# Layer 0's last two experts returned by float32 one-hot products, and layer 1's in-chunk S5 matrix loaded behind its norms

## The chip, the core and the metric

One Trainium2 chip, one of its cores. The time is that of one execution on the device in microseconds (us). TensorE is called PE here (its weight loads PEld), VectorE DVE, ScalarE ACT, GpSimd POOL; SyncE (SP) issues most DMAs. Weights lie in device memory (HBM) and are streamed through SBUF; products are summed in PSUM.

## What is computed

The reference is a two-layer backbone over 256 latent tokens and, in layer 0, 256 context tokens (512 in all, four tiles of 128), 1024 wide:

```
for l in range(2):
    h  = rms_norm(x, norm1_g[l]) * (1 + mod[1]) + mod[0]
    o  = token_mixers(h, ...)            # attention, S5, Fourier: w_in, w_out
    x  = x + mod[2] * o
    h2 = rms_norm(x, norm2_g[l]) * (1 + mod[4]) + mod[3]
    x  = x + mod[5] * moe_ffn(h2)        # 16 experts, each token takes 2
def moe_ffn(t):
    for e in range(16):
        he = silu(t @ w_gate[e]) * (t @ w_up[e])
        y  = y + gates[:, e:e+1] * (he @ w_down[e])
```

What matters here is the end of layer 0's experts (layer 0 handles the context rows as well) and the start of layer 1: x must have both experts' rows, times gate and mod[5], before rms_norm of layer 1 can begin. S5 is a state-space mixer; within chunks of eight time steps it is a product with a fixed matrix made from the layer's S5 parameters.

## The kernel before

The program is written as one stream of instructions in Python; a scheduler sets the order on each engine, by program order among what it expects to be ready, and places the semaphores. `issue_after(x)` binds the instructions of a block to stand behind x on x's own engine. A tile of a pool waits until the last user of its slot is done.

Layer 0's experts are `experts0` (L1569 to L1722). Each expert takes up to 96 gathered tokens ("rows"). For expert e the loop does the gate and up products (eight k-steps, `steps`, out tiles g and u, PE in four column groups), SiLU times up (tile s, L1653 to L1660), three transposes of s (T, L181), a copy to H, and the down product (py, tiles y). The k-steps 0 to 2 of e+1 are put around the transposes of e, so PE has work in the gaps. Each expert's weights come as six pieces of 1 MB (four of gate and up, two of down) that SP issues in order (`wseq`, L1460 and L1463) into nine to thirteen slots; at most eight of these DMAs are under way, each on a semaphore of its own.

Rows go back in this way. Experts 0 to 14: py is copied to y and stored by POOL to a DRAM table Y (L1701, L1702). At the start of expert 15 POOL gathers from Y for each token tile T and for each of the token's two experts the row by an indirect DMA (L1649, eight of them, into weight slots, `rg`). `others(T)` (L1610) scales the two rows by the gates, adds them, multiplies by mod[5] (tile B5) and adds to X[T]: one ACT and three DVE operations, for T = 2 the last two on POOL. Expert 15 itself doesn't go through Y: its rows of Y are zeros (L646), y is split in two float32r halves (`split`), and `combine0` (L1724) returns them by one-hot products with OG, for each T, then times gate and B5 on DVE, added to X. OG is made after expert 14 (L1715 on): a comparison on DVE, a transpose and three small products on PE, two copies on DVE, for each T. `others` for all T stands in program order behind expert 15's y.

`normed` (L397) then takes X[T] tile by tile: square on ACT (L389), a line of DVE, a power on POOL (L394, kept as `self.pow`), the scaling on ACT (L404). `combine0` is called through it, and after each T it also takes steps of `fill`, which loads w_ada and multiplies it (tiles E). Then `mixers(1)` loads w_in (L303) and starts its products A.

Spread over experts 7 to 14 of layer 0, `s5_prep(1)` (L923) makes layer 1's S5 matrices; its in-chunk matrix is written to DRAM (KD) and is to be read back to tile MT by eight DMAs of POOL (`inchunk`, L1051 to L1054, 128 KB each). For layer 1, `inchunk` is called in `mixers` (L508), behind the first projection; nothing binds it to stay there. MT is read in `s5_out`.

Of the kernel before, what the change touches and what calls it, by code (L numbers as in the profile page):

```python
# [14 lines left out]
OP = mybir.AluOpType  # L15
# [119 lines left out]
class Net:  # L135
# [66 lines left out]
    def run(self):  # L202
        nc, A, t = self.nc, self.A, self.t
        with ExitStack() as st:
# [60 lines left out]
            with ExitStack() as s2:  # L265
                last = self.experts0(s2)
            lay.close()
            with ExitStack() as s1:
                with ExitStack() as s2:
                    self.open_psum(s1, s2, 1)  # L270
                    self.open_b(1, "left")
                    self.fill = self.fills(1)
                    self.combine0(*last)
# [133 lines left out]
    def mixers(self, l, sa, sb):  # L407
# [99 lines left out]
        if not both:  # L507
            self.inchunk()  # L508
# [122 lines left out]
        for sh, hp in self.attention(QT, KT, V, MX, BM):  # L631
            if both and sh == 0:
                next(fill, None)
                zi = next(zero, None)
                if zi is not None:
                    nc.gpsimd.dma_start(zi, z[:, None, :].to_broadcast([P, 6, 512]))
            elif both:
                next(nada)
            else:
                next(fill, None)  # L640
                if sh:
                    next(first)
                elif hp == 3:
                    self.fetch(1)
            if both and (sh, hp) == (0, 3):
                nc.gpsimd.dma_start(self.Y[NROW - 96:NROW, :].rearrange("p (a h) -> p a h", a=2),  # L646
                                    z[0:96, None, :].to_broadcast([96, 2, 512]))
# [538 lines left out]
    def route_open(self, l):  # L1186
# [25 lines left out]
        if l == 0:  # L1212
            self.gi = t(pm, [P, 2, nt], "gi", U32)
            self.le = t(pm, [P, 2, nt], "le")
# [22 lines left out]
    def route_tile(self, l, T):  # L1237
# [140 lines left out]
        nc.vector.tensor_copy(self.le[:, 0, T:T + 1], pos[:, NE - 1:NE])  # L1378
        nc.gpsimd.tensor_copy(self.le[:, 1, T:T + 1], GT[:, NE - 1:NE])
# [189 lines left out]
    def experts0(self, st):  # L1569
# [40 lines left out]
        def others(T):  # L1610

            w = rg[T]
            nc.scalar.activation(w[:, 0], w[:, 0], AF.Copy, scale=self.ga[:, 0, T:T + 1])
            nc.vector.scalar_tensor_tensor(w[:, 0], w[:, 1], self.ga[:, 1, T:T + 1], w[:, 0], op0=OP.mult, op1=OP.add)
            v = nc.gpsimd if T == 2 else nc.vector
            v.tensor_tensor(w[:, 0], w[:, 0], B5[T // 2], op=OP.mult)
            v.tensor_tensor(self.X[T], self.X[T], w[:, 0], op=OP.add)
# [9 lines left out]

        xg0, xg = gather(1, nc.sync), None
# [3 lines left out]
        for e in range(NE):  # L1632
# [38 lines left out]
            cp = self.cp(H, pt, 0)  # L1671
            if e == 0:
# [14 lines left out]
            yr = [(slice(0, cap), n, slice(0, YM), slice(512 * n, 512 * n + YM)) for n in range(2)]  # L1687
            yr += [(slice(96, P), n, slice(0, 2 * mt - mt * n), slice(2 * mt * n, 2 * mt + mt * n)) for n in range(2)]
            if e == NE - 1:
# [8 lines left out]
            for i, (r, n, c, d) in enumerate(yr):  # L1698
                self.cp(y[r, d], py[n][r, c], (0, 1, 1, 0)[i])
            Y = self.Y[e * cap:e * cap + cap, :]  # L1700
            nc.gpsimd.dma_start(Y[:, 0:2 * YM].rearrange("r (h c) -> r h c", h=2), y[:cap, :].rearrange("p (h c) -> p h c", h=2)[:, :, 0:YM])  # L1701
            nc.gpsimd.dma_start(Y.rearrange("(b i) c -> i b c", i=32)[:, :, 2 * YM:D],  # L1702
                                y[96:128, 0:3 * mt].rearrange("p (b c) -> p b c", b=3))
            for _ in range(2 if prep else 0):
                with self.tc.issue_after(act.ins), self.tc.issue_after(mul.ins):
                    done = next(prep, prep) is prep
                if done and fin is None:


                    fin = self.fin = self.open(self.finx, "fin", side="right")  # L1710
                    OG = t(fin, [P, 3, 4, P], "OG", F32R)
                    B5 = [self.bcast(fin, "B5", 5, s, 2) for s in range(2)]
                    for T in range(4):
                        og = t(fin, [P, 96], "og")
                        nc.vector.tensor_scalar(og, self.iota, self.le[:, 0, T:T + 1], None, op0=OP.is_equal)  # L1715
                        pt = t(psT, [P, 3, P], "T")
                        self.tr(pt[0:96, 0, :], og)
                        for b in range(3):
                            self.mm(pt[96:128, b, :], og[:, blk(b)], self.ident, True, True)
                        self.cp(OG[0:96, 0, T, :], pt[0:96, 0, :], 0)  # L1720
                        self.cp(OG[96:128, :, T, :], pt[96:128], 0)
        return y, OG, B5  # L1722

    def combine0(self, y, OG, B5):  # L1724

        nc, t = self.nc, self.t

        def add(T):
            mt = D - 2 * YM
            ps = [t(self.psA, [P, YM], "A"), t(self.psA, [P, YM], "A"), t(self.psT, [P, mt], "T")]  # L1730
            for n in range(2):
                for i in range(2):
                    self.mm(ps[n], OG[0:96, 0, T, :], y[i][0:96, 512 * n:512 * n + YM], i == 0, i == 1)
            for b in range(3):
                for i in range(2):
                    self.mm(ps[2], OG[96:128, b, T, :], y[i][96:128, mt * b:mt * b + mt], b + i == 0, b + i == 3)
            for n in range(3):
                c = slice(n * YM, min(n * YM + YM, D))
                w = t(self.tmp, [P, 512], "w2")[:, 0:c.stop - c.start]
                nc.vector.scalar_tensor_tensor(w, ps[n], self.le[:, 1, T:T + 1], B5[T // 2][:, c], op0=OP.mult, op1=OP.mult)  # L1740
                nc.vector.tensor_add(self.X[T][:, c], self.X[T][:, c], w)
            for _ in range((2, 1, 1, 1)[T]):
                next(self.fill)
        self.normed(add)
# [209 lines left out]
```

## Time and profile before

| | us |
|---|---|
| median of 3 runs | 1128.43 (1128.0 to 1131.83) |
| profiled execution, its own time | 1127.95 |
| its span, first to last instruction | 1126.2 |
| PE busy | 1035.6 (92%) |
| DVE busy | 606.4 (54%) |
| ACT busy | 305.5 (27%) |
| POOL busy | 168.9 (15%) |

The profiled execution's own time lies 1.75 us above its span and 0.48 us below the median. All times in rows are counted from the span's start. "[0.46 <-DMA w]" behind a row says that the engine had been idle for 0.46 us before it, and what ended that. A matmul of float32 operands shows as two records, one of float32r operands as one.

### The profile page before, as it was taken

The page shows a single profiled execution, that of the slowest core. Times are in us where ns is not written, and L with a number is a line of the kernel's source. Part 1 is how long each engine was busy: PE and PEld are TensorE (multiplying, and loading weights), DVE is VectorE, ACT ScalarE, POOL GpSimd, SP SyncE. Part 2 cuts the span into 40 slices and gives each one's busy share as a digit, 9 for nine tenths or more (in the row PEclk, how much of TensorE's full clock was granted, in tenths as well). Part 3 has the DMA queues.
Part 4 walks back from the last instruction along what each step waited for, and adds up shares of the span by engine and source line. Part 5 has one row for each costly group of instructions (what it writes and reads, how often), then busy time and mean ns, then how long its engine had stood idle before and what let it go on. Part 6 is the DMA issues. An engine that isn't in the chain of part 4 may idle for free.

```text
span 1126.2 us, 21063 instructions
## 1 busy us (share of the span) xinstructions
PE 1035.6 (92%) x8496; PEld 651.8 (58%) x8496; DVE 606.4 (54%) x1691; ACT 305.5 (27%) x619; POOL 168.9 (15%) x255
## 2 busy tenths in 40 slices
PE   4999998989989999898987889999999899999987
PEld 2667775548885655455654447767558455444533
DVE  8978937568742222297633396695468423232322
ACT  5323234564101111101111136322473221111211
POOL 3101233001223111111220330104010100000000
PEclk9999999999969999999998968999999999999999
DMA  9868576756479999999999646644868899999981
GB/s 312 297 224 220 174 277 249 237 181 243 149 302 278 372 365 377 380 387 372 381 309 367 237 176 243 226 158 161 282 218 294 337 400 401 387 396 403 401 340 40
DMA packets 109393, 325.25 MB, mean 289 GB/s; under 512 B 10704, under 2 KB 19632, under 8 KB 104672
## 3 DMA queue, kind: packets, MB, share of 16 engines
q1 hardware_dynamic: 94464, 276.01, 67.2%
q0 software_dynamic: 14096, 46.57, 12.7%
q8 instruction: 71, 1.16, 0.4%
q10 hardware_dynamic: 720, 1.17, 0.3%
q14 instruction: 42, 0.34, 0.1%
HBM read 305.32 MB, written 18.38 MB: 287 GB/s over the span
## 4 chain that ended last, share of the span: by engine, by line
PE 56%; DMA 23%; DVE 10%; issue 5%; POOL 3%; ACT 3%; SPq 1%; another core or an unknown queue 0%; POOLq 0%; ACTq 0%; DVEq 0%
PE A L157 22%; DMA w<-in_w_up_dram 14%; PE g L157 12%; PE D L157 8%; PE E L157 5%; DMA w<-in_w_gate_dram 5%; PE T L181 4%; PE T L157 2%; PE y L157 2%; DMA w<-in_w_down_dram 1%; PE u L157 1%; POOL qr L752 1%; DMA X<-in_xt_dram 1%; DVE wsp L199 1%; DMA w<-in_w_ada_dram 1%
## 5 line engine op out<-in xcount | busy, mean ns | idle before, releaser
L157 PE MATMUL g<-w,xt 128*32 128x384 f32 (+1 forms) x1280 | 164.4, 456 | 16.4 <-DMA w<-in_w_gate_dram 12.4
L157 PE MATMUL A<-wsp,big 128*128 128x512 f32 (+1 forms) x720 | 161.8, 371 | 3.1 <-DVE big L190 2.0
L157 PE MATMUL u<-w,xt 128*32 128x384 f32 (+1 forms) x1024 | 138.4, 468 | 8.8 <-DMA w<-in_w_up_dram 8.8
L157 PEld LDWEIGHTS A<-wsp,big 128*128 128x128 f32 x720 | 121.1, 188 | 40.1 <-ACT wsp L189 7.5
L157 PEld LDWEIGHTS g<-w,xt 128*32 128x32 f32 x1280 | 70.1, 111 | 63.2 <-issue 33.5
L157 PE MATMUL y<-w,H 128*32 128x384 f32 (+1 forms) x1152 | 89.6, 459 | 1.3 <-DVE H L190 1.3
L157 PE MATMUL g<-w,x 128*64 128x512 f32 x384 | 90.6, 594 | 0.0
L157 PEld LDWEIGHTS u<-w,xt 128*32 128x32 f32 x1024 | 57.5, 112 | 36.7 <-issue 9.8
L157 PE MATMUL E<-w,CS 128*32 128x512 f32 (+1 forms) x448 | 63.2, 589 | 14.4 <-DMA w<-in_w_ada_dram 14.0
L157 PEld LDWEIGHTS y<-w,H 128*32 128x32 f32 x1152 | 52.9, 111 | 34.4 <-issue 12.2
L1893 DVE TENSOR_TENSOR cst<-cst,g 64x512 f32<-64x512 f32 x16 | 11.1, 692 | 111.7 <-ACT cst L1892 111.7
L199 DVE TENSOR_TENSOR wsp<-w,wsp 128x512 fp32r<-128x512 f32 x64 | 43.9, 687 | 44.8 <-ACT wsp L189 43.7
L189 ACT ACTIVATE wsp<-w 128x512 fp32r<-128x512 f32 x64 | 40.4, 631 | 98.8 <-PE A L157 90.3
L157 PE MATMUL A<-w,big 128*128 128x512 f32 (+1 forms) x224 | 67.0, 391 | 0.0
L189 ACT ACTIVATE y<-y 96x384 f32<-96x384 f32 (+4 forms) x34 | 17.9, 531 | 163.2 <-PE y L157 147.4
L1654 DVE TENSOR_TENSOR s<-s,u 96x384 f32<-96x384 f32 x16 | 8.8, 551 | 95.1 <-ACT s L1653 95.0
L157 PEld LDWEIGHTS g<-w,x 128*64 128x64 f32 x384 | 28.7, 137 | 49.9 <-issue 47.8
L1848 DVE SCALAR_TENSOR_TENSOR y<-D,gs,ba 64x256 f32<-64x256 f32 x62 | 30.0, 483 | 45.5 <-PE D L157 44.7
L1598 POOL DMA_DIRECT2D xg<-G x56 | 30.5, 551 | 136.1 <-DVE xt L1605 106.4
L157 PEld LDWEIGHTS A<-w,big 128*128 128x128 f32 x224 | 41.0, 192 | 7.7 <-issue 0.5
L157 PE MATMUL D<-w,WO 128*64 128x256 f32 x352 | 44.2, 393 | 1.1 <-ACT WO L189 1.1
L1892 ACT ACTIVATE cst<-g 64x512 f32<-64x512 f32 x16 | 9.4, 589 | 101.5 <-PE g L157 101.5
(415 smaller groups left out, 1721.8 us busy)
## 6 DMA issues: line engine op xcount, KB each, us to landing
w<-in_w_gate_dram SPq DMA_DIRECT2D x111, 512.0 KB, 13.0
w<-in_w_up_dram SPq DMA_DIRECT2D x111, 512.0 KB, 12.6
w<-in_w_down_dram SPq DMA_DIRECT2D x53, 1024.0 KB, 12.7
w<-in_w_ada_dram SPq DMA_DIRECT2D x27, 1024.0 KB, 6.9
w<-in_w_in_dram SPq DMA_DIRECT2D x14, 1024.0 KB, 5.2
w<-in_w_ada_dram SPq DMA_DIRECT2D x32, 256.0 KB, 6.6
w<-in_w_ada_dram SPq DMA_DIRECT2D x16, 512.0 KB, 4.8
w<-in_w_out_dram SPq DMA_DIRECT2D x8, 1024.0 KB, 7.4
```

The lines of the kernel that those rows point to most:

```text
L157: self.pe = self.pl = self.nc.tensor.matmul(out, lhsT, rhs, start=start, stop=stop)
L181: self.pl = self.nc.tensor.transpose(out, in_, self.ident[:n, :n])
L189: return self.nc.scalar.activation(out, in_, AF.Copy)
L199: self.lo = self.nc.vector.tensor_tensor(lo, x, hi.bitcast(F32), op=OP.subtract)
L752: nc.gpsimd.tensor_tensor(r, v, self.neghalf[:, 0:8], op=OP.pow)
L1598: q.dma_start(xg[blk(g)], rows[g])
L1654: nc.vector.tensor_mul(s[:cap, :], s[:cap, :], pg[1][:cap, 0:384])
L1848: nc.vector.scalar_tensor_tensor(y[o:o + 64, m, b, :], py[m][q, :], gs[q, e % 2:e % 2 + 1], B5[q, m, :], op0=OP.mult, op1=OP.mult)
L1892: nc.scalar.activation(s[64:P], pg[0:64], AF.Silu)
L1893: nc.vector.tensor_mul(s[64:P], s[64:P], pg[64:P])
```

## The change

- At layer 1's `mixers`, `inchunk()` (the eight loads of MT) is bound to stand behind the last `self.pow` on POOL, the power of layer 1's fourth norm.
- Experts 14 and 15 of layer 0 are both kept out of Y: their y stays in SBUF as float32 (`late`), with the last quarter of the columns moved to the same partitions as the rest. Expert 14's two stores on POOL fall away; rows of both experts in Y are zeros, so there is a second zero store early in layer 0.
- OG is float32, two one-hots for each T (one for each of the two experts), with the gate already multiplied in; a transpose each, one copy on ACT for both. The three small products and the DVE copies fall away.
- The gathers thus need Y only up to expert 13. T = 1 takes the slot that T = 3 had. `others(0)` and `others(1)` stand at the start of expert 15; `others(2)` and `others(3)` stand behind expert 15's H copy (DVE) and SiLU (ACT), all on DVE.
- The return products `back(i, T)` (two float32 products of 96 x 128 by 96 x 512, for late expert i = 0, 1): `back(0, 0)` stands on PE between expert 15's up product and the transposes of s, `back(0, 1)` between these and the down product, `back(0, 2)` behind the down product, then `back(1, T)`, with `back(0, 3)` ahead of `back(1, 3)`. DVE multiplies by B5 and adds to X, in two halves of 512.
- `combine0` only keeps the norm and `fill`.

```diff
         if not both:
-            self.inchunk()
+            with self.tc.issue_after(self.pow.ins):
+                self.inchunk()
...
-            self.le = t(pm, [P, 2, nt], "le")
+            self.le = t(pm, [P, nt, 2, 2], "le")
...
-            v = nc.gpsimd if T == 2 else nc.vector
-            v.tensor_tensor(w[:, 0], w[:, 0], B5[T // 2], op=OP.mult)
-            v.tensor_tensor(self.X[T], self.X[T], w[:, 0], op=OP.add)
+            nc.vector.tensor_tensor(w[:, 0], w[:, 0], B5[T // 2], op=OP.mult)
+            nc.vector.tensor_tensor(self.X[T], self.X[T], w[:, 0], op=OP.add)
+
+        def back(i, T):
+
+            for n in range(2):
+                self.mm(acc[T][n], OG[:, i, T, :], late[i][:cap, n * 512:n * 512 + 512], i == 0, i == 1)
...
                 rg = [t(p, [P, 2048], "w").rearrange("p (k n) -> p k n", k=2) for p in (self.ws, self.ws2, self.ws2, self.ws2)]
+                rg = [rg[i] for i in (0, 3, 1, 2)]
                 for T in range(4):
                     for k in range(2):
                         nc.gpsimd.indirect_dma_start(out=rg[T][:, k], out_offset=None, in_=self.Y,
                                                      in_offset=bass.IndirectOffsetOnAxis(ap=self.gi[:, k, T:T + 1], axis=0))
+                for T in range(2):
+                    others(T)
+                acc = [[t(psG, [P, 512], n) for n in "gu"], None, None, None]
...
+            if e == NE - 1:
+                with self.tc.issue_after(self.pe.ins):
+                    back(0, 0)
...
+            if e == NE - 1:
+                acc[1] = [t(psG, [P, 512], n) for n in "gu"]
+                with self.tc.issue_after(self.pl.ins):
+                    back(0, 1)
+                with self.tc.issue_after(cp.ins), self.tc.issue_after(act.ins):
+                    for T in (2, 3):
+                        others(T)
...
-                y = [t(fin, [P, D], f"y{i}", F32R) for i in range(2)]
-                for r, n, c, d in yr:
-                    self.split(y[0][r, d], y[1][r, d], py[n][r, c])
-                with self.tc.issue_after(act.ins), self.tc.issue_after(mul.ins):
-                    for T in range(4):
-                        others(T)
-                break
...
+                late.append(y)
+                for n in range(2):
+                    self.cp(y[:cap, n * YM:n * YM + YM], py[n][:cap, 0:YM], n)
+                for b in range(3):
+                    self.cp(y[blk(b), 2 * YM:D], py[b // 2][96:128, mt * (b % 2):mt * (b % 2) + mt], (0, 1, 1)[b])
...
+                        for i in range(2):
+                            og = t(fin, [P, 96], "og", bufs=2)
+                            nc.vector.tensor_scalar(og, self.iota, self.le[:, T, 0, i:i + 1], self.le[:, T, 1, i:i + 1], op0=OP.is_equal, op1=OP.mult)
+                            self.tr(pt[:cap, i, :], og)
+                        self.cp(OG[:, :, T, :], pt[:cap, 0:2, :], 1)
+
+        acc[2] = [t(psT, [P, 512], "T") for n in range(2)]
+        acc[3] = [t(psY, [P, 512], f"y{n}") for n in range(2)]
+        back(0, 2)
+        for T in range(4):
+            if T == 3:
+                back(0, 3)
+            back(1, T)
             for n in range(2):
...
+                nc.vector.tensor_mul(w, acc[T][n], B5[T // 2][:, c])
                 nc.vector.tensor_add(self.X[T][:, c], self.X[T][:, c], w)
```

## Rows read from the trace of the kernel before

**Rows 1.** The chain that ended last, 540 to 612 us: start, us, what
```profile
556.16 16.38 DMA w<-in_w_gate_dram
...
572.61 24.67 DMA w<-in_w_gate_dram
```

**Rows 2.** Timeline of PE: start, us, what, count, idle before and its releaser
```profile
571.43 0.52 PE L157 MATMUL u<-w,xt 128*32 128x384 f32 x3 [1.38 <-DMA w<-in_w_up_dram]
...
575.95 5.39 PE L157 MATMUL y<-w,H 128*32 128x384 f32 x72
...
597.42 1.50 PE L157 MATMUL g<-w,xt 128*32 128x384 f32 x6 [8.42 <-DMA w<-in_w_gate_dram]
...
604.11 5.39 PE L157 MATMUL y<-w,H 128*32 128x384 f32 x72
```

**Rows 3.** Timeline of POOL, 560 to 650 us: MT's loads, B5, gathers
```profile
572.85 2.82 POOL L1053 DMA_DIRECT2D MT<-KD  x5 [7.23 <-DMA w<-in_w_gate_dram]
...
584.01 1.68 POOL L1053 DMA_DIRECT2D MT<-KD  x3
...
632.67 0.60 POOL L380 DMA_DIRECT2D B<-MD  x1
...
635.98 1.01 POOL L1649 DMA_INDIRECT w<-Y,gi  x1 [2.01 <-PE T L157]
...
644.78 0.94 POOL L1649 DMA_INDIRECT w<-Y,gi  x1 [0.30 <-issue]
```

**Rows 4.** DMA by queue, 576 to 586 us: packets, MB, share of 16 engines
```profile
q1 hardware_dynamic: 360, 1.36, 66.4%
q0 software_dynamic: 239, 0.66, 37.7%
```

**Rows 5.** DMA by queue, 600 to 610 us
```profile
q1 hardware_dynamic: 1076, 4.03, 101.5%
```

**Rows 6.** Timelines of PE and ACT, 629 to 672 us
```profile
629.93 1.09 PE L181 MATMUL T<-cst,LB 128*128 128x128 f32 x8
...
647.69 0.49 ACT L1653 ACTIVATE s<-g 96x384 f32<-96x384 f32 x1 [15.24 <-remote]
...
649.37 0.87 PE L181 MATMUL T<-cst,s 128*128 128x128 f32 x3 [5.34 <-DVE s L1660]
650.89 7.51 PE L157 MATMUL y<-w,H 128*32 128x384 f32 x72 [0.65 <-DVE H L190]
...
670.31 1.06 ACT L389 ACTIVATE w<-X 128x1024 bf16<-128x1024 f32 x1 [9.02 <-DVE X L1741]
```

**Rows 7.** Timeline of DVE: `others(0)`, three operations
```profile
650.87 1.28 DVE L1614 SCALAR_TENSOR_TENSOR w<-w,ga 128x1024 f32<-128x1024 f32 x1
652.18 1.22 DVE L1616 TENSOR_TENSOR w<-w,B 128x1024 f32<-128x1024 f32 x1
653.44 1.23 DVE L1617 TENSOR_TENSOR X<-X,w 128x1024 f32<-128x1024 f32 x1
```

**Rows 8.** Windows: us, busy (count) of PE, PEld, DVE, ACT, POOL; granted clock, DMA share, GB/s
```profile
648.00:658.00 10.00, 7.98 (x74) 4.51 (x75) 8.78 (x10) 4.05 (x6) 0.56 (x1) 0.66 0.51 207
658.00:671.00 13.00, 10.21 (x43) 5.98 (x35) 12.13 (x17) 3.46 (x6) 6.16 (x4) 0.65 0.47 161
```

**Rows 9.** The chain, 1110 to 1126 us: records of whole-array float32 products, 512 wide
```profile
1114.02 1.13 PE A L157 x2
...
1117.24 2.00 PE A L157 x4
```

**Rows 10.** Groups of DVE and timelines, 628 to 690 us: adding to X; norm's end
```profile
L1741 DVE TENSOR_TENSOR X<-X,w 128x384 f32<-128x384 f32 x8 | 4.4, 551 | 0.2
...
673.00 6.32 SPq L303 DMA_DIRECT2D w<-in_w_in_dram  x2
...
681.76 1.15 ACT L404 ACTIVATE U<-X,rstd 128x1024 f32<-128x1024 f32 x1 [0.26 <-POOL rstd L394]
```

More of the change, by code (lines that the diff above doesn't have):

```diff
@@ L265, in run @@
             with ExitStack() as s2:
-                last = self.experts0(s2)
+                self.experts0(s2)
             lay.close()
@@ L272, in run @@
                     self.fill = self.fills(1)
-                    self.combine0(*last)
+                    self.combine0()
                     lay = self.mixers(1, "right", "left")
@@ L645, in mixers @@
             if both and (sh, hp) == (0, 3):
-                nc.gpsimd.dma_start(self.Y[NROW - 96:NROW, :].rearrange("p (a h) -> p a h", a=2),
-                                    z[0:96, None, :].to_broadcast([96, 2, 512]))
+                for i in (1, 2):
+                    nc.gpsimd.dma_start(self.Y[NROW - 96 * i:NROW - 96 * i + 96, :].rearrange("p (a h) -> p a h", a=2),
+                                        z[0:96, None, :].to_broadcast([96, 2, 512]))
         if both:
@@ L1376, in route_tile @@
             return
-        nc.vector.tensor_copy(self.le[:, 0, T:T + 1], pos[:, NE - 1:NE])
-        nc.gpsimd.tensor_copy(self.le[:, 1, T:T + 1], GT[:, NE - 1:NE])
+        nc.vector.tensor_copy(self.le[:, T, 0, :], pos[:, NE - 2:NE])
+        nc.gpsimd.tensor_copy(self.le[:, T, 1, :], GT[:, NE - 2:NE])
         IN, SL = t(bc, [P, NE], "IN"), t(bc, [P, NE], "SL")
@@ L1626, in start @@
             return steps, pg, lambda k: w[k // 2][:, k % 2, :]
+        late = []
         xg0, xg = gather(1, nc.sync), None
@@ L1686, in experts0 @@
             mt = D - 2 * YM
-            yr = [(slice(0, cap), n, slice(0, YM), slice(512 * n, 512 * n + YM)) for n in range(2)]
-            yr += [(slice(96, P), n, slice(0, 2 * mt - mt * n), slice(2 * mt * n, 2 * mt + mt * n)) for n in range(2)]
-            if e == NE - 1:
-                y = [t(fin, [P, D], f"y{i}", F32R) for i in range(2)]
-                for r, n, c, d in yr:
-                    self.split(y[0][r, d], y[1][r, d], py[n][r, c])
-                with self.tc.issue_after(act.ins), self.tc.issue_after(mul.ins):
-                    for T in range(4):
-                        others(T)
-                break
-            y = t(ex, [P, D], "y")
[L1698 to L1703, printed above, removed]
+            y = t(ex, [P, D], "y")
+            if e < NE - 2:
+                yr = [(slice(0, cap), n, slice(0, YM), slice(512 * n, 512 * n + YM)) for n in range(2)]
+                yr += [(slice(96, P), n, slice(0, 2 * mt - mt * n), slice(2 * mt * n, 2 * mt + mt * n)) for n in range(2)]
+                for i, (r, n, c, d) in enumerate(yr):
+                    self.cp(y[r, d], py[n][r, c], (0, 1, 1, 0)[i])
+                Y = self.Y[e * cap:e * cap + cap, :]
+                nc.gpsimd.dma_start(Y[:, 0:2 * YM].rearrange("r (h c) -> r h c", h=2), y[:cap, :].rearrange("p (h c) -> p h c", h=2)[:, :, 0:YM])
+                nc.gpsimd.dma_start(Y.rearrange("(b i) c -> i b c", i=32)[:, :, 2 * YM:D],
+                                    y[96:128, 0:3 * mt].rearrange("p (b c) -> p b c", b=3))
+            else:
+                late.append(y)
[3 more added lines that the diff above has]
+                    self.cp(y[blk(b), 2 * YM:D], py[b // 2][96:128, mt * (b % 2):mt * (b % 2) + mt], (0, 1, 1)[b])
             for _ in range(2 if prep else 0):
@@ L1710, in experts0 @@
                     fin = self.fin = self.open(self.finx, "fin", side="right")
-                    OG = t(fin, [P, 3, 4, P], "OG", F32R)
+                    OG = t(fin, [cap, 2, 4, P], "OG")
                     B5 = [self.bcast(fin, "B5", 5, s, 2) for s in range(2)]
                     for T in range(4):
-                        og = t(fin, [P, 96], "og")
-                        nc.vector.tensor_scalar(og, self.iota, self.le[:, 0, T:T + 1], None, op0=OP.is_equal)
                         pt = t(psT, [P, 3, P], "T")
[L1717 to L1730, printed above, removed]
-            for n in range(2):
[L1732 to L1740, printed above, removed]
+                        for i in range(2):
+                            og = t(fin, [P, 96], "og", bufs=2)
+                            nc.vector.tensor_scalar(og, self.iota, self.le[:, T, 0, i:i + 1], self.le[:, T, 1, i:i + 1], op0=OP.is_equal, op1=OP.mult)
+                            self.tr(pt[:cap, i, :], og)
@@ new lines, in experts0 @@
+                        self.cp(OG[:, :, T, :], pt[:cap, 0:2, :], 1)
[6 more added lines that the diff above has]
+            back(1, T)
+            for n in range(2):
+                c = slice(n * 512, n * 512 + 512)
+                w = t(self.tmp, [P, 512], "w2")
+                nc.vector.tensor_mul(w, acc[T][n], B5[T // 2][:, c])
@@ L1741, in add, with combine0, ready @@
                 nc.vector.tensor_add(self.X[T][:, c], self.X[T][:, c], w)
+    def combine0(self):
+        def ready(T):
             for _ in range((2, 1, 1, 1)[T]):
                 next(self.fill)
-        self.normed(add)
+        self.normed(ready)
         self.finx.close()
```

## The prediction

> **What bounds the kernel now.** I read the chain of waits first, from 540 to 700 us, since the page's shares are means over stages with different limits. Two places on it concern this change.
>
> From 556 us the chain runs over weight transfers; one takes 24.67 us from its issue, where the one before took 16.38 [rows 1]. PE stands still for 8.42 us until the first piece of expert 14 is there [rows 2]. In that time the POOL queue moves MT, issued at 572.85 and 584.01 [rows 3]. From 576 to 586 us the weight queue moved 1.36 MB and the POOL queue 0.66 [rows 4]; undisturbed, the weight queue moves 4.03 MB in 10 us [rows 5]. So MT is paid for in weights, where weights are what PE waits for.
>
> The second place is the joint between the layers. Expert 14's down product ends at 629.93, the first norm begins at 670.31: 40.4 us [rows 6]. In them expert 15 needs 17.8 us to its SiLU, then its down product runs 7.51 us (5.39 in [rows 2]), at a mean clock of 0.66, between the two granted levels of 1.2 and 2.4 GHz [rows 8]. Gathers start only at 635.98 and go on to 645.7 in their issue alone [rows 3]. From 658 to 671 DVE is busy 12.13 of 13 us [rows 8]: the four `others`, y's halves and the additions all come there. So the joint is bound by what was put off to its end, not by PE.
>
> **The change part by part.** *MT's move.* Lost weights from 576 to 586 are 4.03 - 1.36 = 2.67 MB, 6.6 us at the rate of [rows 5]; the three loads issued from 584.01 act again. PE's own loss is the 8.42 us and the slow restart: from 597.42 to the down product at 604.11 are 6.69 us, where expert 13 took 4.52 plus some 0.25 done before its wait [rows 2]. Together 8.42 + 1.9 = 10.3 us at most. Without MT the first pair of expert 14 comes 6.3 MB of weights and 0.4 MB of stores behind that of expert 13, which ended a wait at 571.43; 6.7 MB at 403 GB/s are 16.6 us, 588.1, and PE is ready at 589.0 (597.42 - 8.42). So nearly all is gained; I take 9.5, bounds 7 and 10.3. Behind it PE is its own bound, and SP's later loads wait for PE's slots and shift with it.
>
> At its new place MT's eight issues (4.5 us) stand behind the last power; behind them on POOL come only loads and powers of the projections, tens of us later. Its transfers fall beside w_in's second half and the next w_ada. These are issued at 679.3 and later, when the norms end at 682.91 [rows 10]; in the new order PE's backlog is shorter and slots come free earlier, so I take 1 us, bounds 0 and 7 (the 6.6 us above and a rest).
>
> The Trainium skill (DMA: Bandwidth & Descriptors, Queues, rings and completion order) says that each DMA engine takes turns among the queues with work, packet by packet. The trace agrees: two queues share the engines 66.4 to 37.7 [rows 4]. By that rule MT costs weights wherever a weight load is under way: it is the first rival below.
>
> *The joint.* Count from expert 14's last down product. PE: LB's transposes 1.1 [rows 6]; 90 records of gate and up left, at 5.39/72 each, 6.7 [rows 2]; eight transposes of one-hots, a third of a T row's 0.87 each at most [rows 6], 1.2 taken; waits between DVE, PE and ACT for the one-hots 2, taken (0 to 6: before, the same stretch took 17.8 us for at most 11 of work, and its last 3.6 us have no row). Expert 15's SiLU thus starts at 11.0 instead of 17.8.
>
> Then s needs 1.7 us (647.69 to 649.37), filled by `back(0, 0)`. A return product is two records: (2.00 - 1.13)/2 = 0.435 us each [rows 9], so 0.87, and 1.74 for a `back`. Transposes 0.87; `back(0, 1)` 1.74 covers the H copy, 0.65 (650.24 to 650.89) [rows 6]; down product 5.39 [rows 2], since PE has no gap in which the clock falls: 11.0 + 1.74 + 0.87 + 1.74 + 5.39 = 20.7. `others(2)` and `others(3)` are 3.73 us each on DVE [rows 7] and start with the H copy's end at 14.3, so DVE comes to y at 21.8; its part, 1 us, is done at 22.8, behind `back(0, 2)` at 22.5. `back(1, 0)` ends at 24.5. DVE then has a multiplication and an addition of 512; 0.551 for 384 [rows 10] gives 0.7 each: first norm at 25.9, against 40.4. Later T come each 1.74 us of PE and 2.8 of DVE, the last behind two `back`; before, the four norms take 12.6 us, 670.31 to 682.91 [rows 6, 10], 3.15 each, so PE and DVE stay ahead. `others(0)` and `others(1)`, 7.5 us on DVE, lie beside the gate and up products; they need B5, which can be issued when LB is done, and T = 0 and 1, gathered before expert 14 has ended because their slots are free and Y is only needed to expert 13. The gain is 14.5, bounds 8 (waits of 6 and DVE late) and 18 (no waits).
>
> The Trainium skill (Perfetto Trace Analysis, Engine Utilization) rates the array at 307.2 G outputs a second, halved for FP32_LOW_HIGH. By it a product of 128 x 512 would take 0.43 us, an estimate; the rows show 0.87 for its two records, so the row decides. By the page's figure the first norm would come some 0.9 us earlier.
>
> *The rest.* Expert 14's two stores fall away, the second zero store is one POOL issue of about 0.6 us early in layer 0, beside attention; the two-column copies for `le` cost the same. I take nothing; if that cover is gone it is under 1 us.
>
> Sum: 1127.95 - 9.5 - 14.5 + 1 = 1104.95, say **1105** (the profiled execution's own time; the median lies 0.48 above it). Everything behind the joint shifts as it is: its loads wait on its own slots.
>
> **The rivals.** *MT holds up layer 1.* At the new place the weight queue gets a third of its rate for some 10 us; if w_in's second half or w_ada is still under way, PE waits up to 7 us. For it: two w_in loads are only just issued at the norms' start [rows 10]. Against: PE needs the second half four k-steps later. 1105 + 6 = 1111.
>
> *The one-hots and DVE stay the bound.* DVE runs in order; if `others(0)` waits for B5 ahead of one-hots or of s, PE waits too, and PE's 3.6 us without a row may return. 1105 + 6 = 1111.
>
> *Only one half works.* The gathers stay behind B5 on POOL, as at 632.67 and 635.98 [rows 3], and the joint gains 5 instead of 14.5, or the weights come late without MT too: 1114.
>
> *Slower.* DVE's order is the mechanism: if all four `others` (15 us) stand ahead of s, PE is idle for 15 us from 11.0 on, the clock goes to its lower level, and products behind it (8 x 1.74 + 5.39 = 19.3 us) take twice that: 15 + 19.3 = 34 over the plan, 10 beyond both gains: 1139. It decides from some 24 us of loss. Against: two of the four are bound behind the H copy.
>
> **How the numbers follow.** Forecast 0.58; MT in layer 1 0.16; one-hots and DVE 0.15; one half 0.07; slower 0.04. The forecast's own range is 1098 (10.3 and 18 gained, 1 given back, 1127.95 - 27.3 = 1100.65, less 2.65 for loads that start sooner) to 1109; rivals reach 1114, and with the bounds 7, 8 and 7 together 1120. I leave the corners out: 1098 to 1116. A measurement of this kernel tells about 0.5% (5.6 us) from no change; faster by more is under 1122.8: 0.93, within it 0.03, slower 0.04.
>
> **What would show it.** Right: no POOL MT row before the norms of layer 1; no PE wait of several us at expert 14; four of the gathers issued before expert 14's down product ends; the down product of expert 15 near 5.4 us at full clock; about 26 us from expert 14's last product to the first norm; A products following U's scaling by the 3 us of before. Wrong: PE waits for w_in or w_ada behind the norms, DVE idle in front of `others(0)` with one-hots behind it, or expert 14 still waiting for weights.

## The result, and the profile after

| | kernel before | kernel after |
|---|---|---|
| median (range), us | 1128.2 (1125.7 to 1131.8, 4 runs) | 1111.6 (1109.2 to 1114.4, 4 runs) |
| ratio, 95% interval | 1 | 0.9844 (0.9808 to 0.988) |
| profiled execution: time, span, us | 1127.95, 1126.2 | 1112.08, 1110.3 |

Faster by 16.6 us, inside the range, 6.6 us above the forecast of 1105. The sum is close for a wrong reason: one of its two large terms was a little too small, the other has no shown gain behind it, and in the profiled pair differences between two executions fill the gap.

The timeline of PE in the kernel after (start, us, what, count, idle before and its releaser), from expert 12's down product to expert 15's, against [rows 2] and [rows 6]:

```profile
573.60 5.41 PE L157 MATMUL y<-w,H 128*32 128x384 f32 x72
...
591.19 5.41 PE L157 MATMUL y<-w,H 128*32 128x384 f32 x72
...
611.71 5.39 PE L157 MATMUL y<-w,H 128*32 128x384 f32 x72
617.03 1.09 PE L181 MATMUL T<-cst,LB 128*128 128x128 f32 x8
618.05 0.83 PE L157 MATMUL g<-w,xt 128*32 128x384 f32 x2
622.91 0.42 PE L181 MATMUL T<-cst,og 128*96 128x128 f32 x1 [4.03 <-DVE og L1738]
...
635.20 1.13 PE L157 MATMUL g<-y,OG 96*128 96x512 f32 x2
...
640.03 5.41 PE L157 MATMUL y<-w,H 128*32 128x384 f32 x72
...
648.43 1.02 PE L157 MATMUL g<-y,OG 96*128 96x512 f32 x2
649.29 1.02 PE L157 MATMUL u<-y,OG 96*128 96x512 f32 x2
```

No wait for weights is left: expert 13's product stands 12.9 us earlier than at 604.11 [rows 2], expert 14's ends at 617.1 instead of 630. But behind it PE waits 4.03 us for a one-hot, and expert 15's product comes 22.9 us behind the end of expert 14's; 20.9 before.

POOL, ACT and DVE in the kernel after say why (same columns; a w read from Y is a gathered row block, og a one-hot):

```profile
610.27 1.43 POOL L1658 DMA_INDIRECT w<-Y,gi  x1 [10.99 <-DMA w<-in_w_down_dram]
...
618.41 0.61 POOL L380 DMA_DIRECT2D B<-MD  x1
...
664.86 4.53 POOL L1055 DMA_DIRECT2D MT<-KD  x8
```

```profile
616.40 1.15 ACT L1615 ACTIVATE w<-w,ga 128x1024 f32<-128x1024 f32 x1 [8.02 <-DMA w<-Y,gi]
617.79 1.15 ACT L1615 ACTIVATE w<-w,ga 128x1024 f32<-128x1024 f32 x1 [0.25 <-issue]
619.67 0.88 ACT L189 ACTIVATE y<-y 96x384 f32<-96x384 f32 x2 [0.73 <-PE g L157]
...
634.88 0.49 ACT L1665 ACTIVATE s<-g 96x384 f32<-96x384 f32 x1 [3.20 <-PE g L157]
...
656.57 1.06 ACT L389 ACTIVATE w<-X 128x1024 bf16<-128x1024 f32 x1 [9.20 <-DVE X L1753]
...
664.94 1.15 ACT L404 ACTIVATE U<-X,rstd 128x1024 f32<-128x1024 f32 x1 [0.26 <-POOL rstd L394]
```

```profile
620.34 1.28 DVE L1616 SCALAR_TENSOR_TENSOR w<-w,ga 128x1024 f32<-128x1024 f32 x1 [7.03 <-DMA w<-Y,gi]
621.54 0.98 DVE L190 COPY y<-y 96x384 f32<-96x384 f32 x2
622.45 0.55 DVE L1738 TENSOR_SCALAR og<-cst,le 128x96 f32<-128x96 f32 x2
...
645.95 1.00 DVE L190 COPY y<-y 96x384 f32<-96x384 f32 x2
...
655.25 1.29 DVE L1753 TENSOR_TENSOR X<-X,w 128x512 f32<-128x512 f32 x2
```

MT's loads have left the expert stage and stand behind the last power (664.86; 572.85 in [rows 3]). The gathers now stand ahead of B5, 26 us earlier than in [rows 3], yet the first starts only at 610.27, and the first rows are there at 616.4. On ACT and DVE `others(0)` stands **ahead** of y's copies and of the one-hots, and these engines run in order: DVE does nothing from 613.3 to 620.34, and the one-hots that PE needs come behind it. One thing more holds y's copies up in this execution: ACT is free from 618.94 and waits until 619.67 for PE, though the product has ended at 617.1. The second execution of this kernel (experiment 2) doesn't have that, and has the same wait for `others(0)`. Windows of the kernel after (columns as in [rows 8]) show the second half of the price:

```profile
618.00:623.00 5.00, 0.97 (x5) 0.26 (x3) 2.65 (x6) 3.27 (x6) 3.41 (x5) 0.97 0.98 362
623.00:627.00 4.00, 4.00 (x20) 1.17 (x20) 1.76 (x4) 0.38 (x1) 2.04 (x1) 0.61 1.00 389
```

PE is busy 0.97 of 5 us, and in the next four the granted clock is 0.61, near its lower level of 1.2 GHz. Expert 15's SiLU, at 634.88, is 17.8 us behind expert 14's product (17.7 before), the first norm 39.5 us (40.3). Only the norms are shorter, 9.5 us instead of 12.6: they end at 666.09 instead of 682.91 [rows 10].

### The profile page after: what moved, and what is told of

It is laid out like the page before. It is cut to its first block, busy times and chain, and to the rows that moved or that the text cites. A ratio compares the mean times of both kernels' runs of the same rounds, so it can differ in the third digit from the quotient of the medians.

```text
span 1110.3 us, 20995 instructions
## 1 busy us (share of the span) xinstructions
PE 1034.4 (93%) x8468; PEld 650.3 (59%) x8468; DVE 601.7 (54%) x1679; ACT 306.4 (28%) x623; POOL 166.6 (15%) x252
## 4 chain that ended last, share of the span: by engine, by line
PE 60%; DMA 18%; DVE 11%; issue 4%; ACT 4%; POOL 2%; SPq 1%; POOLq 0%; DVEq 0%; ACTq 0%
PE A L157 22%; DMA w<-in_w_up_dram 14%; PE g L157 13%; PE D L157 8%; PE E L157 5%; PE T L181 4%; PE u L157 3%; PE y L157 2%; PE T L157 2%; DMA w<-in_w_down_dram 1%; POOL qr L754 1%; DMA X<-in_xt_dram 1%; DVE wsp L199 1%; DMA G<-h,si 1%; ACT E L817 1%
## 5 line engine op out<-in xcount | busy, mean ns | idle before, releaser
L157 PE MATMUL g<-w,xt 128*32 128x384 f32 (+1 forms) x1280 | 161.2, 455 | 9.3 <-DMA w<-in_w_gate_dram 5.6
L157 PEld LDWEIGHTS A<-wsp,big 128*128 128x128 f32 x720 | 122.5, 191 | 41.2 <-ACT wsp L189 7.5
L157 PE MATMUL u<-w,xt 128*32 128x384 f32 (+1 forms) x1024 | 135.6, 473 | 4.6 <-DMA w<-in_w_up_dram 4.6
L157 PE MATMUL y<-w,H 128*32 128x384 f32 (+1 forms) x1152 | 86.9, 451 | 0.8 <-DVE H L190 0.7
L157 PE MATMUL E<-w,CS 128*32 128x512 f32 (+1 forms) x448 | 58.5, 559 | 13.3 <-DMA w<-in_w_ada_dram 13.3
L1909 DVE TENSOR_TENSOR cst<-cst,g 64x512 f32<-64x512 f32 x16 | 11.1, 692 | 110.1 <-ACT cst L1908 110.1
L189 ACT ACTIVATE wsp<-w 128x512 fp32r<-128x512 f32 x64 | 40.4, 632 | 100.1 <-PE A L157 91.9
L189 ACT ACTIVATE y<-y 96x384 f32<-96x384 f32 (+2 forms) x34 | 17.6, 517 | 146.2 <-PE y L157 126.1
```

What stands on the lines that cost most here:

```text
L157: self.pe = self.pl = self.nc.tensor.matmul(out, lhsT, rhs, start=start, stop=stop)
L189: return self.nc.scalar.activation(out, in_, AF.Copy)
L1909: nc.vector.tensor_mul(s[64:P], s[64:P], pg[64:P])
```

## The experiments

Runs that stand under one number ran on one chip, beside the kernel before; its median there is given, because it differs (1122 to 1129 us). Ratios are compared, not times; a ratio on record can lie some 0.001 from the quotient of the two medians. "Joint" is from the end of expert 14's down product; "norms done" is the end of U's scaling.

**1. The two parts alone, and two suspected orders** (before: 1122.5 us, 18 runs).

MT alone, in the kernel before:

```diff
         if not both:
-            self.inchunk()
+            with self.tc.issue_after(self.pow.ins):
+                self.inchunk()
```

> The kernel before with MT's eight loads alone moved behind the last power of layer 1's norms; nothing of the joint is changed. By the prediction's own term (9.5 us gained, 1 given back) 1119.7 us against 1128.2. By the trace of after, where expert 14's down product ends 12.8 us earlier (617.1 instead of 629.9) and PE waits 0.7 us for w_ada behind the norms: about 1115.5, and PE without any wait of several us at expert 14. If MT holds up layer 1 in its new place, 1121 or more, with PE waits for w_in or w_ada behind the norms.

Measured: 1111.1 us, ratio 0.9909 (0.9877 to 0.994): 10.2 us gained by the ratio, and no wait of PE for weights at expert 14.

The joint alone, the kernel after with that hunk taken back:

> The kernel after with MT's loads put back to their old place; the joint is that of after. By the prediction (joint 14.5 us) 1113.7 us. By the reading of after's trace, where expert 14's last product to the first norm is still 39.5 us (40.4 before) and only the norms are shorter (9.5 us for 12.6): 1124 us. PE waits some 8 us for expert 14's first weights again in both.

Measured: 1123.6 us, ratio 1.0007 (0.9985 to 1.0028). The joint alone gains nothing; a gain over 1.7 us lies outside the interval. Both theories of the expectation gave it too much (14.5 and 4 us).

The weighted sums behind the one-hots (`lastog`, `lastOG`: the last og on DVE, its last copy on ACT):

```diff
-                for T in range(2):
-                    others(T)
+                with self.tc.issue_after(lastog.ins), self.tc.issue_after(lastOG.ins):
+                    for T in range(2):
+                        others(T)
```

> The kernel after with others(0) and others(1) bound behind the last one-hot on DVE and the last copy of one-hots on ACT. Theory 1 (the two weighted sums stand ahead of y's copies and the one-hots and wait for gathers; PE idles 4.0 us and then runs 3 us at the low clock): PE's wait at 618.9 goes, expert 15's SiLU comes 11 to 12 us after expert 14's down product instead of 17.8, and the time is 1105. Theory 2 (DVE's sum of work is the bound of the joint: others(0) and others(1), 7.5 us, now lie between one-hots and s, so that s waits for them): the SiLU comes earlier, but s only 2 to 3 us earlier, time 1108.5 to 1109.5. Theory 3 (the gathers' arrival alone): no change, 1111.6.

Measured: 1111.4 us (1104.2 to 1114.7), ratio 0.9899 (0.9863 to 0.9934). ACT, DVE and PE of this kernel:

```profile
625.36 0.49 ACT L1666 ACTIVATE s<-g 96x384 f32<-96x384 f32 x1 [2.42 <-PE g L157]
```

```profile
626.60 2.35 DVE L1618 TENSOR_TENSOR X<-X,w 128x1024 f32<-128x1024 f32 x2
628.99 0.55 DVE L1667 TENSOR_TENSOR s<-s,u 96x384 f32<-96x384 f32 x1
```

```profile
608.88 5.39 PE L157 MATMUL y<-w,H 128*32 128x384 f32 x72
...
630.05 0.44 PE L181 MATMUL T<-cst,s 128*128 128x128 f32 x2 [2.38 <-DVE s L1673]
```

The SiLU comes 11.1 us behind the product (614.27 to 625.36), the prediction's 11.0, with PE busy 12.0 of the 12 us from 614 to 626 at a clock of 1.00: theory 1's mechanism. But s then waits on DVE until the two sums are done (theory 2): expert 15's product ends at 24.2 instead of 28.3. The profiled execution took 1105.2 us, the median shows no gain against the kernel after (0.9902, below).

The returns' products in buffers of their own:

```diff
-                w = t(self.tmp, [P, 512], "w2")
+                w = t(fin, [P, 512], "wr", bufs=2)
                 nc.vector.tensor_mul(w, acc[T][n], B5[T // 2][:, c])
```

> The kernel after with the returns' products w in two buffers of their own instead of those that the norms' squares write to as well. If the shared buffers hold back the first square until the seventh product is added (656.57, X of T = 0 being ready at 651): the first squares come at about 651, and the layer starts earlier by 2 to 3 us, not by all 5.6, since DVE has the first variance only behind the returns in its order: 1109. If ACT or X were what the square waits for: no change, 1111.6.

Measured: 1113.2 us, ratio 0.9907 (0.9875 to 0.994). ACT and DVE of this kernel:

```profile
652.35 1.06 ACT L389 ACTIVATE w<-X 128x1024 bf16<-128x1024 f32 x1 [3.66 <-DVE X L1753]
```

```profile
658.38 0.20 DVE L391 TENSOR_SCALAR var<-ss 128x1 f32<-128x1 f32 x2
```

The first square starts 33.2 us behind the product instead of 39.5, so the shared buffer, `w2`, was what it waited for. Its variance stands behind the returns on DVE all the same (658.38), and the norms are done at 45.4 instead of 49.0. The time shows none of it.

**2. Both kernels once more, and the orders together** (before: 1122.8 us, 11 runs).

> The changed kernel itself once more, beside the kernel before on this chip. If the two parts add as the runs with one part alone say (MT alone 0.991, the joint alone 1.001 of the kernel before): 0.991 to 0.992. If the joint is worth the few microseconds that the first pair of traces leaves for it: 0.984.

Measured: 1110.4 us, ratio 0.9902 (0.9877 to 0.9927). As the two parts alone say; less than in the first comparison, whose interval ends below this one's middle. PE, POOL, ACT and DVE of this execution:

```profile
607.38 5.39 PE L157 MATMUL y<-w,H 128*32 128x384 f32 x72
```

```profile
605.94 1.43 POOL L1658 DMA_INDIRECT w<-Y,gi  x1 [10.99 <-PE u L157]
```

```profile
612.76 2.33 ACT L1615 ACTIVATE w<-w,ga 128x1024 f32<-128x1024 f32 x2 [8.71 <-DMA w<-Y,gi]
615.12 0.87 ACT L189 ACTIVATE y<-y 96x384 f32<-96x384 f32 x2
```

```profile
615.21 1.28 DVE L1616 SCALAR_TENSOR_TENSOR w<-w,ga 128x1024 f32<-128x1024 f32 x1 [6.23 <-DMA w<-Y,gi]
616.41 0.99 DVE L190 COPY y<-y 96x384 f32<-96x384 f32 x2
```

Here PE's update for the product that ends at 612.77 comes at once (0.02 us behind it by the trace's semaphore events), and y's copies begin only when `others(0)` and `others(1)` let them: on ACT 2.4 us behind the product, on DVE 3.6. The gather row says what its slot waited for: PE, which had just done the first k-steps of expert 15 (around 14's transposes).

> The kernel before once more, one look, for what stands between expert 14's down product and the first norm. In the trace that the prediction read, PE stands still for some 5 us from about 643, 3.6 of them without a row; with MT moved alone the same code has no such gap and expert 15's SiLU comes 12.3 us after expert 14's product instead of 17.8. If the gap belongs to the kernel (or to MT's place): 17 to 18 us again. If it was that one execution's: 12 to 13 us, the first norm 34 to 35 us after the product, and a time some 5 us below 1128.

Measured: 1121.2 us. ACT of the kernel before, in the execution of the prediction and in this one:

```profile
647.69 0.49 ACT L1653 ACTIVATE s<-g 96x384 f32<-96x384 f32 x1 [15.24 <-remote]
```

```profile
642.20 0.49 ACT L1653 ACTIVATE s<-g 96x384 f32<-96x384 f32 x1 [9.88 <-PE g L157]
```

The same windows of 5 us ahead of that SiLU, in the execution of the prediction and in this one:

```profile
643.00:648.00 5.00, 0.81 (x3) 0.25 (x3) 0.85 (x2) 0.31 (x1) 2.11 (x4) 1.00 0.94 333
```

```profile
636.00:641.00 5.00, 4.84 (x58) 3.17 (x59) 2.29 (x6) 0.00 (x0) 3.78 (x5) 1.00 0.88 271
```

The trace shows nothing that released the first ("remote": no record of this core). So 5.4 us of the 40.3 that the prediction set out to shorten, up to the SiLU, belong to that one execution (called its standstill below): with the same instructions the SiLU comes 12.3 us behind expert 14's product and the first norm 34.6, here and with MT alone.

The three orders together: the two edits above, and the additions moved into `ready(T)`, so that each variance is traced right behind its block:

```diff
     for T in range(4):
         ...
         back(1, T)
-        for n in range(2):
-            ...
+    def add(T):
+        for n in range(2):
+            ...
+    return add
...
         def ready(T):
+            add(T)
```

> The kernel after with three edits of order: others(0) and others(1) behind the one-hots, the returns' products in buffers of their own, and each row block's additions traced ahead of that block's norm so that DVE has its variance between them. Theory (the joint is bound by DVE's order and work): expert 14's product to the last scaling of the norms takes 38 to 40 us, where after has 49 and the one with the first edit alone 44.9; time 5 to 7 us under after's. Rival (ACT or PE bound): no better than the first edit alone, 3 to 4 us under after's.

Measured: 1107.6 us, ratio 0.987 (0.9849 to 0.9892), 2.9 us under the kernel after beside it, with intervals that overlap. The norms are done at 41.2 (50.0 in the kernel after beside it), but from there to the end it takes 447.5 us (445.0). SyncE's queue and ACT of this kernel, and a window:

```profile
651.29 1.23 SPq L303 DMA_DIRECT2D w<-in_w_in_dram  x2
```

```profile
660.45 0.63 ACT L189 ACTIVATE wsp<-w 128x512 fp32r<-128x512 f32 x1 [3.74 <-DMA w<-in_w_in_dram]
```

```profile
655.00:665.00 10.00, 6.68 (x31) 4.90 (x32) 4.75 (x9) 5.59 (x11) 3.54 (x7) 0.60 1.05 244
```

w_in's loads have not moved forward as far as the norms have: the first of these is issued 36.2 us behind expert 14's product, 40.7 in the kernel after beside it (4.5 us against 8.8 for the norms). Layer 1 waits for them, and the clock falls to 0.60; ten microseconds at the same distance from the norms (661.5 to 671.5) have 0.83 in the kernel after beside it.

> The same as the run before it, and the products with B5 and the additions of others(1) and others(2) on POOL, 5.1 us each there, instead of DVE, 2.4 us each. If DVE's sum of work bounds the joint: s waits 2 us less for DVE and the whole is another 2 to 4 us shorter. If the gathers' arrival or PE bound it: no change against the run before it; if POOL becomes late: 2 us longer.

```diff
-            nc.vector.tensor_tensor(w[:, 0], w[:, 0], B5[T // 2], op=OP.mult)
-            nc.vector.tensor_tensor(self.X[T], self.X[T], w[:, 0], op=OP.add)
+            v = nc.gpsimd if T in (1, 2) else nc.vector
+            v.tensor_tensor(w[:, 0], w[:, 0], B5[T // 2], op=OP.mult)
+            v.tensor_tensor(self.X[T], self.X[T], w[:, 0], op=OP.add)
```

Measured: 1111.5 us, ratio 0.9896 (0.9875 to 0.9916), 3.9 us over the run before it; norms done at 45.5. POOL and DVE:

```profile
634.49 3.35 POOL L1618 TENSOR_TENSOR w<-w,B 128x1024 f32<-128x1024 f32 x1 [2.39 <-DVE w L1616]
637.92 3.23 POOL L1619 TENSOR_TENSOR X<-X,w 128x1024 f32<-128x1024 f32 x1
```

```profile
635.64 3.29 DVE L1618 TENSOR_TENSOR w<-w,B 128x1024 f32<-128x1024 f32 x1
638.97 3.27 DVE L1619 TENSOR_TENSOR X<-X,w 128x1024 f32<-128x1024 f32 x1
```

DVE's own product lasts 3.29 us beside POOL's where it took 1.22 in [rows 7], and each ends 1.1 us behind POOL's (638.93 behind 637.84; 642.24 behind 641.15). POOL's product in turn lasts 3.35 us where one of this shape took 2.38 in the kernel before (at 658.40); DVE's operation ahead of it ends at 635.61, 1.1 us after POOL's start:

```profile
633.13 2.48 DVE L1616 SCALAR_TENSOR_TENSOR w<-w,ga 128x1024 f32<-128x1024 f32 x2
```

What was to be taken off DVE came back as waiting.

**3. MT later in layer 1** (before: 1129.4 us, 11 runs). MT's loads some 45 us later, behind the first power of the q and k norms:

```diff
-            with self.tc.issue_after(self.pow.ins):
-                self.inchunk()
+            self.pend = self.inchunk
...
-        nc.gpsimd.tensor_tensor(r, v, self.neghalf[:, 0:8], op=OP.pow)
+        qpow = nc.gpsimd.tensor_tensor(r, v, self.neghalf[:, 0:8], op=OP.pow)
+        if self.pend:
+            with self.tc.issue_after(qpow.ins):
+                self.pend()
+            self.pend = None
```

> The three edits of order (others(0) and others(1) behind the one-hots, buffers of their own for the returns' products, additions traced ahead of each norm), and MT's eight loads some 43 us later in layer 1, behind the first power of the q and k norms, long before MT is first read (71 us behind the norms in after). In the run with the three edits alone the norms ended 41.2 us after expert 14's product (49.0 in after), but from there to the end took 447.5 us instead of 444.2, with scalar-engine waits for w_in and a clock of 0.64. If MT's transfers beside w_in take that back: from the last scaling to the end 444 us, time 3 us under the run with the three edits. If not (w_in's loads are simply issued too late for the earlier norms): no change, 447.5.

Measured: 1107.0 us, ratio 0.9801 (0.977 to 0.9831), the lowest of all.

> The three edits of order once more, for a comparison with the run before it on one chip: 0.987 of the kernel before, as it measured.

Measured: 1114.4 us, ratio 0.986 (0.9827 to 0.9892). ACT of this execution, where the product ends at 618.69, so that y's copies come 2.5 us behind it with no sum in front:

```profile
621.22 0.88 ACT L189 ACTIVATE y<-y 96x384 f32<-96x384 f32 x2 [11.26 <-PE g L157]
```

> The kernel after with only MT's loads put later, as in the run with the late loads. What MT costs beside layer 1's first loads in the kernel after: by the prediction 1 us (0 to 7); by the traces, where from the last scaling to the end takes 444.2 to 445.2 us in the joint of after with MT either behind the norms or in its old place, nothing: 0.990 to 0.991 of the kernel before.

Measured: 1109.3 us, ratio 0.9814 (0.9789 to 0.9838). ACT's wait for w_in in the first of the three:

```profile
662.04 0.63 ACT L190 ACTIVATE wsp<-w 128x512 fp32r<-128x512 f32 x1 [2.13 <-DMA w<-in_w_in_dram]
```

The wait is 2.13 us instead of 3.74, and layer 1's first store to MD comes 42.3 us behind the norms instead of 46.4. To the end, however, it is 447.2 against 447.5, and of the 4.7 us between the two spans (1106.6 and 1111.3) 4.3 are there at the end of expert 14's product already (614.35 and 618.69), where the kernels don't differ. The medians are 7.4 us apart, the intervals touch: late loads are at least no worse, the traces do not show where 7 us would come from. The kernel after with late loads does as well as the three orders with them; so the orders, worth 5 to 9 us at the joint, are not shown to be worth anything at the end.

**4. MT alone, at the late place, in the kernel before** (before: 1125.3 us, 9 runs).

> The kernel before with MT's eight loads alone moved, to the late place in layer 1 (behind the first power of the q and k norms); the joint is the old one. If the whole gain of the change is MT's and the new joint adds nothing: 0.988 to 0.991 of the kernel before, as MT alone behind the norms had (0.991) or a little under it, since from the last scaling to the end took 442.6 us there and 442.3 with late loads. If the new joint brings something that the runs so far hide: 0.995 or more.

Measured: 1109.8 us, ratio 0.9862 (0.9839 to 0.9885). One moved load, with the old joint, does as much as the whole change did in both comparisons (0.9844 and 0.9902). The kernel after with late loads had 0.9814 on another chip, its interval just below this one; so with late loads a few microseconds for the new joint are not excluded by the times, though its trace doesn't show them (next table).

The joint in all kernels, each from one profiled execution (us behind the end of expert 14's product; last column from the norms to the end):

| kernel | SiLU of 15 | product of 15 done | first square | norms done | rest |
|---|---|---|---|---|---|
| before (prediction) | 17.7 | 28.4 | 40.3 | 52.9 | 443.3 |
| before (2) | 12.3 | 20.6 | 34.6 | 47.2 | 442.4 |
| MT alone | 12.3 | 22.2 | 34.6 | 47.2 | 442.6 |
| MT alone, late | 12.3 | 20.5 | 34.6 | 47.2 | 443.6 |
| after | 17.8 | 28.3 | 39.5 | 49.0 | 444.2 |
| after (2) | 18.2 | 28.8 | 39.9 | 50.0 | 445.0 |
| joint alone | 17.0 | 27.6 | 38.7 | 48.6 | 445.2 |
| after, MT late | 18.7 | 29.2 | 40.4 | 50.3 | 442.3 |
| own buffers | 17.0 | 27.6 | 33.2 | 45.4 | 447.8 |
| sums behind one-hots | 11.1 | 24.2 | 35.4 | 44.9 | 444.1 |
| three orders | 11.1 | 24.2 | 29.8 | 41.2 | 447.5 |
| three orders (again) | 15.0 | 28.2 | 33.8 | 45.1 | 447.5 |
| three orders, MT late | 15.0 | 28.2 | 33.8 | 45.1 | 447.2 |
| three orders, POOL | 11.1 | 25.2 | 33.9 | 45.5 | 447.1 |

The last two columns together are the way from expert 14's product to the end of the kernel: 489.6 to 490.8 us for the old joint in its three executions without the standstill, 492.6 to 495.0 for the new one in four, 488.7 to 492.6 for the three orders in their three (without POOL).

## Why the prediction was right in sign and sum, and wrong in its terms

**MT's move: right mechanism, mis-sized term.** Forecast 9.5 (7 to 10.3). From the start of expert 12's down product to the end of expert 14's the three traces with MT's loads there take 54.1 (575.95 to 630.00 [rows 2]), 54.8 and 55.5 us, all eleven without them 43.5 (573.60 to 617.10 in the kernel after): 10.6 to 12.0 us, over the upper bound. That bound was PE's wait of 8.42 us and the restart behind it in one execution; in the two others the wait alone is 9.48 and 8.54. By the ratio of MT alone it is 10.2 us, interval 6.7 to 13.8. Expert 14's product ends 12.9 to 13.0 us earlier in the pairs of traces, but 1.7 to 2.4 of that are there at the start of expert 12's product already, and come from before MT's loads: with MT alone the 1.7 stand at expert 12's SiLU (568.92 and 570.57; MT's first issue in the second execution of before is at 574.25), and in the first pair most is PE's wait of 1.38 us that ends at 571.43 [rows 2], ahead of 572.85. A wait of 1.32 us stands in the same place in a trace with MT moved (MT alone, late).

**MT in layer 1: within bounds by the traces, open by the times.** Forecast +1 (0 to 7). From the norms to the end MT alone takes 442.6 us against 442.4 and 443.3 without it there; in the kernel after 444.2 and 445.0, with late loads 442.3, but the joint alone, which has no MT there, 445.2. So a cost between -1 and 3 us, with 0.8 to 0.9 between two executions of one kernel. The times leave more room: the kernel with late loads always has the lower ratio (0.9862 and 0.9909 with the old joint, 0.9814 and 0.9844 or 0.9902 with the new, 0.9801 and 0.986 with the three orders: 3 to 10 us), though only the last pair is from one chip, and there the intervals touch. So the rival with 6 us of loss is neither seen in a trace nor excluded; a wait for w_in shows when the norms come earlier, as in the three orders.

**The joint: the term that failed.** Forecast -14.5 to the first norm (8 to 18). In the first pair it went from 40.3 to 39.5, and 3.1 us more come from shorter norms. Against executions of the old joint without the standstill the new one is longer: norms done at 48.6 to 50.3 in four traces, 47.2 in three of the old. Four steps failed.

- *The base.* The prediction noted that the last 3.6 of expert 15's 17.8 us "have no row" and took them as something that the new order removes. They were no part of the kernel: 12.3 us in the next execution, and in both with MT alone moved. A loss without a row needs a second execution before it becomes a gain. (A slip beside it: of the four `others` the first was done at 654.67 [rows 7], ahead of the 13 us in which the prediction has all four.)
- *"Gathered before expert 14 has ended because their slots are free."* Five gathers are issued before 617.1, as forecast, but the first only at 610.27 and its rows are there at 616.4. The slots were not free: in both traces of the kernel after the first gather starts 0.27 us behind PE's update for the first k-steps of expert 15 (610.00 and 605.67), 6.8 us ahead of the end of expert 14's down product, and the row that DVE waits for comes with the third gather, issued at 613.73 and landed at 620.26. The cost of that is DVE's and ACT's order, which the prediction had as its second rival with 1111 us ("if `others(0)` waits ... ahead of one-hots"), though for B5 and not for gathers. Shown by the runs with the sums behind the one-hots: SiLU at 11.1 in three traces, no idle PE, clock 1.00, against 17.0 to 18.2 in three with the sums ahead. In the others PE's update for expert 14's product is late (below), and the same order makes 15.0 (two traces) of 17.8 and 18.7. But for that order, the forecast's path to the SiLU, 11.0, was right.
- *"`others(0)` and `others(1)`, 7.5 us on DVE, lie beside the gate and up products."* Their rows come too late for that. Put behind the one-hots, they stand ahead of s: DVE comes to s only at 628.99 in the run of experiment 1, PE waits 2.38 us for it, and expert 15's product ends at 24.2 instead of the forecast's 20.7. This is theory 2, and most of what keeps the first square of the three orders at 29.8 instead of 25.9.
- *The end.* "First norm at 25.9" took the first norm to be free once its X is added. The squares wrote into the same two buffers as the returns' products, and the variance stood behind all returns on DVE: 5.6 us passed from X's last addition for T = 0, about 651.0, to the first square at 656.57. Shown for the buffer by the run with buffers of their own, for the order by the three orders (first square 29.8).

Terms of that path which held: expert 15's product 5.41 us at a clock of 1.00 (forecast 5.39); return products 0.86 us apart (forecast 0.87), of which the rows at 648.43 and 649.29 of PE's timeline are a pair; DVE done with y 11.8 us behind the SiLU as forecast (22.8 less 11.0), 12.1 measured.

**Why the sum held.** By luck, as far as the profiled pair shows. Between the two profiled executions of the first comparison 2.35 us are gained up to expert 12's product, where MT has no part, 10.55 from there to the end of expert 14's (MT), 3.9 at the joint (52.9 to 49.0: 5.7 of the standstill, less 1.8 that the new joint is longer), and 0.9 lost behind it: 15.9 of the span, of which some 8 are differences between two executions. In the second comparison the change is worth 11 us (0.9902), and the forecast's 23 would have been twice the gain.

**What stays open.** What the late updates of PE come from. In the first trace of before PE's last rows end at 644.0 and what waits for them goes on at 647.7. In four of the ten traces with the new joint (after, after with MT late, three orders again and with MT late) the update for expert 14's product comes 2.4 to 2.5 us behind its end, in the other six 0.02; y's copies, which need it, wait, PE then idles for the one-hots, and its clock falls (0.61 in after, 0.66 from 622 to 627 in the three orders again). In the trace of after, the five updates that lie 0.02 to 1.80 us behind that product in the second trace of after come 2.46 to 2.66 us behind it, all within 0.2 us, while the rows of the work in question start at 617.03 and 618.05: there the updates were late rather than the work. All of these lie beside the gathers, with the DMA engines 0.94 to 0.98 busy, but so do executions without lateness. No experiment took the gathers away, and whether the other runs of the first comparison had the standstill no profile shows. Open too is where the kernels with late loads gain the time that their traces don't show.

## What to carry over

A wait or a gap without a releaser in one profiled execution is not yet a cost of the kernel; look for it in a second execution before it is put into a sum. Where work is hoisted to an earlier place, ask not only when its data come but what stands behind it on its in-order engine; a wait that was off the path there can hold up what is on it. And a chain of earlier steps is worth its length only as far as the transfers of the next stage move forward with it: here norms that came 8.8 us earlier met w_in's loads, which came 4.5 us earlier. Before a difference at one place is given to an edit, look whether it was there ahead of the edited place: 1.7 to 2.4 of the 13 us at expert 14 were.

## What the runs showed of the hardware

POOL's two-input operations and DVE's held each other up: with POOL's product of 128x1024 running from 634.49 to 637.84, DVE's, started 1.15 us later, ended 1.09 us behind it and took 3.29 us instead of 1.22. The Trainium skill (SBUF — State Buffer, Who interferes with whom) says that a DVE instruction with two inputs in SBUF and a GpSimd instruction that reads SBUF share a port pair, locked for a whole instruction; the trace agrees in both pairs of rows, and it fits that work moved from DVE to POOL gained nothing (0.9896 against 0.987).

The kernel before took 1122 to 1129 us by chip, in groups of 9 to 18 runs of one chip each, more than any edit of order changed; so kernels are compared here by their ratios to the kernel before of the same group.
